# Attention over latent keys: who turns the exponentials, and a pool of large buffers cut in two

## The chip, the cores and the metric

The kernel runs on one core of a Trainium2 chip. The metric is the device time of one execution in microseconds (us); lower is better. All data are float32. For the large products an operand is split into two float32r parts, high and low (`hi = round(x)`, `lo = x - hi`), and a product is made of three matmuls: hi by hi, hi by lo, lo by hi.

The engines, by the names that the profile uses: PE (TensorE, matmuls; PEld is its loading of weights), DVE (VectorE), ACT (ScalarE), POOL (GpSimd), SP (SyncE, which issues most DMAs here). Each takes its own instructions strictly in the planned order. PSUM holds what TensorE writes; SBUF holds the tiles that the others work on; DRAM is reached by DMA only.

## What is computed

One layer of a diffusion backbone over 1024 latent tokens and 256 context tokens of width 1024: a SwiGLU FFN, then a short convolution beside grouped-query attention, merged and projected, then a second FFN, each with a modulated RMS norm. The change lies in the attention of the latent tokens, cut here to what matters:

```python
N_Q_HEADS, N_KV_HEADS, HEAD_DIM, SEQ, CTX_LEN = 8, 2, 128, 1024, 256

def gqa_attend(q, k, v):
    s = jnp.einsum('btkgd,blkd->bkgtl', q, k, preferred_element_type=jnp.float32) * (HEAD_DIM ** -0.5)
    p = jax.nn.softmax(s, axis=-1).astype(v.dtype)
    return jnp.einsum('bkgtl,blkd->btkgd', p, v)

k_all = jnp.concatenate([k_c, k_l], axis=1)   # 256 context keys, then 1024 latent keys
v_all = jnp.concatenate([v_c, v_l], axis=1)
o_l = latent_attention(q_l, k_all, v_all)     # 128 queries at a time
```

Per head and query there are 1280 keys: ten blocks of 128, two of the context and eight latent ones.

## The kernel before, in words

**Stages.** The first FFN (in a Winograd-like form that makes seven products of eight), the mixed projections, heads (q, k, v with norm and rotary), the attention stage, the merge and output projection, the second FFN, the final norm. A planner orders each engine's instructions: it takes the program's order as priority, but when an instruction isn't ready by its estimate of the times, a later one that is ready goes first. Waits are put in afterwards.

**Units.** Attention works in 16 units, one for each of 8 heads and 2 halves of the queries (512 each, four tiles `qt` of 128). `Unit.scores(qt)` makes the scores of one query tile: queries on the partitions, keys along the row, 256 of the context into half a bank and two banks of 512 for the latent keys. VectorE takes the row maxima (`m`, `nm`), ScalarE writes the exponentials, for the context into `pc` and for the latent keys into a tile `pl` of [128, 1024] for each query tile, and their sums into `rs`, which VectorE adds up into `rsum`.

**The second product.** It contracts over the keys, so the exponentials must have keys on the partitions. `Unit.turn(kt)` does that for one key block: four TensorE transposes, one for each query tile, into one PSUM bank `pt`; then `split` makes the two parts in a tile `pts` (ScalarE's cast for the high part, VectorE's subtraction for the low one). `Unit.values(kt, pts)` adds three matmuls of 512 columns to the bank `po`. `Unit.inverse` (at the fifth value step) takes the reciprocals of the sums and brings them, by two DMAs of POOL's queue through DRAM (`rinvd`, `rrow`), into a row that stands on all partitions. `Unit.output` copies `po` and lets POOL multiply it by that row.

**The order.** `seconds()` is a generator over all units and key blocks: each step turns one block, and once more than AHEAD (3) turned blocks wait, it multiplies the oldest. The loop over `units[1:]` issues a unit's `scores` and between them ten steps of the previous unit (`run(rest, 1)`), and steps of `fillers()`: the convolution branch's output projection (`conv_out`, with weights `wc` loaded and split by `conv_weights`, the subtraction on POOL), which is used up after about eleven units. In the last three units `split_output` puts casts and subtractions (`oh`, `ol`) of finished heads on POOL. After the loop the remaining steps run beside the first `merge` steps.

**Buffers.** Large tiles (4 KB on each partition) come from one pool of A_BUFS = 38 slots (`atile`): the residual stream, kept operands, k, v, q, the exponentials `pc` and `pl`, and so on. Split weights and `pts` take turns in four slots of the tag `wh`; small [128, 512] tiles come from `ttile` (11 slots).

A helper class records all engine calls, so that nearly all rows of the profile have the line L90; the names of the tiles tell them apart.

Of the kernel before, what the change touches and what calls it, by code (L numbers as in the profile page):

```python
# [37 lines left out]
A_BUFS = 38  # L38
W_BUFS = 4
AHEAD = 3  # L40
# [11 lines left out]
def tile_dit_layer(  # L52
# [52 lines left out]
    dram = ctx.enter_context(tc.tile_pool(name="dram", bufs=1, space=DRAM))  # L105

# [6 lines left out]
    def atile(name, shape=(P, SLOT), dt=F32):  # L113
        return apool.tile(list(shape), dt, tag="A", name=uniq(name))

# [291 lines left out]
    class Latents:  # L407


        def __init__(self, name):  # L410
            self.name, self.t = name, {}

        def pair(self, k, i):
            if (k, i) not in self.t:
                self.t[k, i] = atile(self.name, (P, 2, 512))
            return self.t[k, i]
# [6 lines left out]
    class Context:  # L423
        def __init__(self, name, dt=F32):
            self.t = [atile(name, (P, 4, CT), dt) for _ in range(2)]
# [66 lines left out]
    class Winograd:  # L492
# [6 lines left out]
        def __init__(self, xs, gain, mod, m, pairs, plain=False, ahead=3, side_from=None):  # L499
# [12 lines left out]
            self.source, self.ready = self.lefts(pairs, side_from), []  # L512

        def keep(self, i, k, src, lo_eng=None):

            t = atile(f"r{i}", (P, 2, 512), F32R)
            split(src, t[:, 0], t[:, 1], lo_eng)
            self.r[i][k] = t
# [38 lines left out]
        def norm1(self, turned=None):  # L557
# [8 lines left out]
            def scaled(k):  # L566
                t22[k] = ttile("h22")
                if self.plain:
                    self.r[0][k] = atile("h12", (P, 2, 512))
                    t12[k] = self.r[0][k][:, 0]  # L570
# [26 lines left out]
        def part_second(self, k):  # L597

            t = self.r[0][k]
            h = atile("r0", (P, 2, 512), F32R)  # L600
            split(t[:, 0], h[:, 0], h[:, 1])
# [133 lines left out]
        def start_by_half(self):  # L735

            uc = [atile("uc", (P, 2, 512)) for _ in range(2)]
# [96 lines left out]
    def row_products(w, rows, add, after=lambda i, k: None, halves=False):  # L834
# [12 lines left out]
        s1, s2, w11 = {}, {}, {}  # L847
# [13 lines left out]
        def parts(src, where):  # L861
# [3 lines left out]
            else:  # L865
                if where == "kept":
                    t = atile("kept", (P, 2, 512), F32R)
# [19 lines left out]
        def second_sum(k, m):  # L887
            s2[k] = atile("ws", (P, 2, 512))[:, :m]
# [3 lines left out]
        def sums(i, g):  # L892
# [11 lines left out]
            if i == 1 and g >= 3 or i == 4 and g < n - 3:  # L904
                k, m = groups[g - 3 if i == 1 else n - 3 + g]
                s1[k] = atile("ws", (P, 2, 512))[:, :m]
# [94 lines left out]
    xs, xc = Latents("x"), Context("xc")  # L1001

    def fetch_tokens(ch):
# [3 lines left out]
        for j in range(n // P):  # L1007
            t = atile("xtok")
# [166 lines left out]
    def side(j, bank=ps_o):  # L1175
        pc = bank()

        def do(i, w):
# [9 lines left out]
            if i == 4:  # L1188
                if j % 2 == 0:
                    hid_c[j // 2] = atile("hidc", (P, 4, CT), F32R)  # L1190
# [45 lines left out]
    for j in range(NH):  # L1236
# [6 lines left out]
        if j == SIDE_FROM - 1:  # L1243
# [10 lines left out]
            for token in range(2):  # L1254
                c_acc.append(atile("cacc"))
# [31 lines left out]
    xs = Latents("x1")  # L1287
# [116 lines left out]
    rope_t = [atile("rope", (P, KD, HD)) for _ in range(2)]  # L1404
    for i in range(2):
        sp.dma_start(out=rope_t[i][:], in_=rope[i])
    hg = atile("hg", (P, 2, HD))
# [171 lines left out]
    class Unit:  # L1579
# [3 lines left out]
        def begin(self):  # L1583
# [3 lines left out]
            self.pl = []  # L1587
            self.rsum = small("rsum", 4)

        def scores(self, qt):  # L1590
# [7 lines left out]
            m3, nm, rs = small("m3", 3), small("nm", 1), small("rs", 3)  # L1598
            dve.reduce_max(out=m3[:, 0:1], in_=sx, axis=AX.X)
            if self.hd == 0 and self.ch[1] == 0 and qt < 2:  # L1600
                pl = wpool.tile([P, SLOT], F32, tag="raw", name=uniq("pl"), bufs=3)
            else:
                pl = atile("pl")
            self.pl.append(pl)
            for j in range(2):
# [4 lines left out]
                parts.append((pl[:, j * 512 : (j + 1) * 512], ps))  # L1610
            dve.tensor_reduce(out=nm[:], in_=m3[:], axis=AX.X, op=ALU.max, negate=True)
            for j, (dst, ps) in enumerate(parts):
                act.activation(out=dst, in_=ps, func=AF.Exp, bias=nm[:], accum_out=rs[:, j : j + 1])
            dve.reduce_sum(out=self.rsum[:, qt : qt + 1], in_=rs[:], axis=AX.X)

        def turn(self, kt):

            pt = ps_t()
            for qt in range(4):
                src = self.pc[:, qt, kt * P : (kt + 1) * P] if kt < 2 else self.pl[qt][:, (kt - 2) * P : (kt - 1) * P]  # L1620
                transpose(pt[:, qt * P : (qt + 1) * P], src)
            pts = wpool.tile([P, 2, 512], F32R, tag="wh", name=uniq("pts"), bufs=W_BUFS)
            split(pt, pts[:, 0], pts[:, 1])
# [11 lines left out]
        def inverse(self):  # L1635
            rinv = small("rinv", 4)
# [6 lines left out]
        def output(self):  # L1643
            of = q_of(self.hd, self.ch)
            act.copy(out=of, in_=self.po)
            pool.tensor_mul(out=of, in0=of, in1=self.rows)

    def seconds():

        turned = []  # L1650
# [9 lines left out]
        for u in units:  # L1660
            for kt in range(10):
                turned.append((u, kt, u.turn(kt)))
# [3 lines left out]
        while turned:  # L1666
# [6 lines left out]
    def merge(j, ch):  # L1673

        if j not in m_hi:
            m_hi[j], m_lo[j] = atile("mh", dt=F32R), atile("ml", dt=F32R)
# [18 lines left out]

# [216 lines left out]
```

## Time and profile before

Three runs: 2631.09, 2631.25 and 2631.54 us, median 2631.25 us. The profiled execution:

| | |
|---|---|
| span | 2631.1 us |
| PE busy | 99% |
| DVE / ACT / POOL busy | 76% / 45% / 21% |
| granted TensorE clock | 0.998 |
| first and last transpose of `pl` start | 1462.6 us, 1808.7 us |
| number of `pl` transposes | 512 |
| number of splits into `pts` | 160 |
| DMA, mean over the span | 146 GB/s |

A row of instructions reads: line, engine, operation, output <- inputs by the program's names, shape, count | busy us, mean ns of one | idle time of the engine just before them, and what ended it. A row of the timeline reads: start (us), duration (us), engine, line, operation, output <- inputs, count, and in brackets the idle time before. PE durations run from issue to a modelled end and overlap; the distance from start to start is the slot that an instruction takes.

### The profile page before, as it was taken

The page shows a single profiled execution, that of the slowest core. Times are in us where ns is not written, and L with a number is a line of the kernel's source. Part 1 is how long each engine was busy: PE and PEld are TensorE (multiplying, and loading weights), DVE is VectorE, ACT ScalarE, POOL GpSimd, SP SyncE. Part 2 cuts the span into 40 slices and gives each one's busy share as a digit, 9 for nine tenths or more (in the row PEclk, how much of TensorE's full clock was granted, in tenths as well). Part 3 has the DMA queues.
Part 4 walks back from the last instruction along what each step waited for, and adds up shares of the span by engine and source line. Part 5 has one row for each costly group of instructions (what it writes and reads, how often), then busy time and mean ns, then how long its engine had stood idle before and what let it go on. Part 6 is the DMA issues. An engine that isn't in the chain of part 4 may idle for free.

```text
span 2631.1 us, 35379 instructions
## 1 busy us (share of the span) xinstructions
PE 2609.9 (99%) x12665; PEld 2176.1 (83%) x12665; DVE 1997.4 (76%) x3360; ACT 1183.5 (45%) x2343; POOL 545.8 (21%) x425
## 2 busy tenths in 40 slices
PE   8999999999999999999999999999999999999998
PEld 5888899888888888888888888888888888888888
DVE  5888976877897879977788576676457886667996
ACT  6533454333454642333355566574237333334553
POOL 0133201221010034333022112132000442321100
PEclk9999999999999999999999999999999999999999
DMA  8665465345973365542522322113425653227831
GB/s 324 205 210 182 149 215 173 106 131 185 327 184 117 124 205 160 163 134 89 200 77 85 86 87 65 33 37 118 158 85 176 201 167 96 90 80 286 191 84 65
DMA packets 372905, 384.69 MB, mean 146 GB/s; under 512 B 19686, under 2 KB 256376, under 8 KB 372728
## 3 DMA queue, kind: packets, MB, share of 16 engines
q1 hardware_dynamic: 363288, 363.52, 42.1%
q0 software_dynamic: 9440, 18.91, 4.3%
q8 instruction: 99, 1.62, 0.2%
q14 instruction: 78, 0.64, 0.1%
HBM read 310.45 MB, written 71.86 MB: 145 GB/s over the span
## 4 chain that ended last, share of the span: by engine, by line
PE 94%; DVE 3%; DMA 1%; ACT 1%; issue 1%; SPq 0%; DVEq 0%; ACTq 0%
PE ps L90 81%; PE pt L90 8%; PE po L90 6%; DMA rawm<-in_w_mod_dram 1%; DVE xb L90 0%; DVE wl L90 0%; DVE macc L90 0%; DVE m L90 0%; DVE y L90 0%; DVE pts L90 0%; DMA xtok<-in_x_dram 0%; DVE x L90 0%; DVE r L90 0%; SPq L90 0%; DVE rs_t L90 0%
## 5 line engine op out<-in xcount | busy, mean ns | idle before, releaser
L90 PE MATMUL ps<-r,wl 128*128 128x512 f32 x5196 | 1198.3, 390 | 3.6 <-ACT r L90 1.3
L90 PEld LDWEIGHTS ps<-r,wl 128*128 128x128 f32 x5196 | 972.4, 188 | 207.7 <-ACT r L90 1.6
L90 ACT CAST wl<-sum 128x512 fp32r<-128x512 f32 x218 | 134.1, 622 | 294.4 <-PE ps L90 227.1
L90 ACT CAST wl<-raw 128x512 fp32r<-128x512 f32 x287 | 178.2, 622 | 193.1 <-PE ps L90 147.9
L90 DVE TENSOR_TENSOR wl<-raw,wl 128x512 fp32r<-128x512 f32 x287 | 210.2, 736 | 61.0 <-ACT wl L90 59.3
L90 DVE TENSOR_TENSOR wl<-sum,wl 128x512 fp32r<-128x512 f32 x218 | 196.9, 904 | 33.5 <-ACT wl L90 32.3
L90 POOL TENSOR_TENSOR sum<-raw 128x512 f32<-128x512 f32 x55 | 76.4, 1389 | 680.6 <-DMA raw<-in_ffn_w_in_dram 345.3
L90 DVE SCALAR_TENSOR_TENSOR macc<-rawm,silu_c,macc 128x512 f32<-128x512 f32 x178 | 145.4, 835 | 17.1 <-DMA rawm<-in_w_mod_dram 16.6
L90 DVE TENSOR_TENSOR u<-u,ps 128x512 f32<-128x512 f32 x186 | 126.5, 680 | 32.2 <-PE ps L90 32.1
L90 ACT CAST rh<-hid 128x512 fp32r<-128x512 f32 x132 | 82.2, 623 | 139.4 <-PE ps L90 112.3
L90 POOL TENSOR_TENSOR sum<-raw,sum 128x512 f32<-128x512 f32 x55 | 76.7, 1395 | 287.0 <-DVE wl L90 284.0
L90 DVE TENSOR_TENSOR pts<-pt,pts 128x512 fp32r<-128x512 f32 x160 | 107.3, 686 | 36.2 <-ACT pts L90 34.6
L90 DVE TENSOR_REDUCE m<-ps 128x1 f32<-128x256 f32 (+1 forms) x192 | 111.0, 597 | 29.4 <-PE ps L90 28.5
L90 ACT CAST pts<-pt 128x512 fp32r<-128x512 f32 x160 | 92.2, 597 | 85.5 <-PE pt L90 84.4
L90 PE MATMUL ps<-rh,wl 128*128 128x512 f32 x360 | 122.8, 390 | 0.0
L90 PE MATMUL ps<-wh,r 128*128 128x512 f32 x384 | 120.7, 392 | 0.0
L90 DVE TENSOR_TENSOR rl<-hid,rh 128x512 fp32r<-128x512 f32 x132 | 91.0, 693 | 29.9 <-ACT rh L90 19.4
L90 ACT CAST wh<-raw 128x512 fp32r<-128x512 f32 (+1 forms) x85 | 68.2, 803 | 95.5 <-PE ps L90 74.9
L90 PE MATMUL ps<-kl,qs 128*128 128x512 f32 x384 | 104.0, 394 | 0.1
L90 PE MATMUL ps<-rh,wh 128*128 128x512 f32 x300 | 102.8, 389 | 0.0
L90 PE MATMUL ps<-y,wc 128*128 128x512 f32 x384 | 95.3, 391 | 0.2 <-DVE g L90 0.2
L90 POOL TENSOR_TENSOR sum<-sum,raw 128x512 f32<-128x512 f32 x55 | 87.8, 1597 | 5.7 <-PE ps L90 3.9
(325 smaller groups left out, 5102.3 us busy)
## 6 DMA issues: line engine op xcount, KB each, us to landing
raw<-in_ffn_w_in_dram SPq DMA_DIRECT2D x131, 512.0 KB
raw<-in_ffn_w_out_dram SPq DMA_DIRECT2D x72, 512.0 KB
raw<-in_w_in_dram SPq DMA_DIRECT2D x64, 512.0 KB
rawm<-in_w_mod_dram SPq DMA_DIRECT2D x104, 256.0 KB
hid<-hd SPq DMA_DIRECT2D x40, 512.0 KB
ucd<-uc SPq DMA_DIRECT2D x33, 512.0 KB
rawm<-in_w_mod_dram SPq DMA_DIRECT2D x32, 512.0 KB
ws<-in_ffn_w_out_dram POOLq DMA_DIRECT2D x26, 512.0 KB, 6.4
```

Of the source, the lines that this page charges most:

```text
L90: inst = getattr(self.engine, name)(*args, **kw)
```

## The change

The exponentials of the latent keys are no longer turned by TensorE.

- `Unit.begin` takes two tiles `pl` of [128, 2048], one for each half of the latent keys. The exponentials are written so that in each tile 32 keys of query tile 0 are followed by the same 32 keys of query tiles 1, 2 and 3, then the next 32 keys.
- `Unit.bring(kt)`: for the two context blocks the four TensorE transposes as before. For every second latent block one VectorE transpose in place over [128, 1024], which turns each 32x32 block by itself; four SP DMAs (one for each 32 partitions) write the result to a DRAM tile in pieces of 128 floats; and for each block one SP DMA reads 256 KB back into a `ttile`, now with keys on the partitions.
- `Unit.turn(kt, pt)` makes the split. For the context blocks the casts and subtractions reorder the columns as well; for the latent blocks they read SBUF, and the subtractions of blocks 3, 5, 6, 7 and 9 are on POOL.
- `seconds()` has one more queue: more than BROUGHT (3) blocks are brought before the oldest is split, and AHEAD is 2.
- The four sums `rsum` are made by one VectorE instruction in `inverse`; `output` copies with reordered columns.
- The pool of 38 slots becomes one of 30 and a second of 8, in the memory of which four slots of 8 KB (for `pl`) lie during attention (`share`). Outside attention a number of tiles take their slots from the second pool by name (`btile` in place of `atile`); in the mixed stage two `h12` share one tile.

```diff
-A_BUFS = 38
+A_BUFS, B_BUFS, Q_BUFS = 30, 8, 4
 W_BUFS = 4
-AHEAD = 3
+AHEAD = 2
+BROUGHT = 3
...
+    def share(tag, bufs):
+
+        if shared:
+            shared.pop("guard").__exit__(None, None, None)
+        guard = tc.tile_pool(name=uniq("share"), bufs=bufs, reuse_waits="tile")
+        shared.update(guard=guard, pool=guard.__enter__(), tag=tag)
...
+    def btile(name, shape=(P, SLOT), dt=F32):
+        return shared["pool"].tile(list(shape), dt, tag=shared["tag"], name=uniq(name))
...
             self.pc = atile("pc", (P, 4, CT))
-            self.pl = []
-            self.rsum = small("rsum", 4)
+            self.pl = [btile("pl", (P, 2048)) for _ in range(2)]
+            self.done = 0
+            self.rs, self.rsum = small("rs", 12), small("rsum", 4)
...
-                parts.append((pl[:, j * 512 : (j + 1) * 512], ps))
+                pl = self.pl[j][:].rearrange("p (b q c) -> p b q c", q=4, c=32)
+                parts.append((pl[:, :, qt], ps.rearrange("p (b c) -> p b c", c=32)))
...
-                act.activation(out=dst, in_=ps, func=AF.Exp, bias=nm[:], accum_out=rs[:, j : j + 1])
-            dve.reduce_sum(out=self.rsum[:, qt : qt + 1], in_=rs[:], axis=AX.X)
-
-        def turn(self, kt):
-
-            pt = ps_t()
-            for qt in range(4):
-                src = self.pc[:, qt, kt * P : (kt + 1) * P] if kt < 2 else self.pl[qt][:, (kt - 2) * P : (kt - 1) * P]
-                transpose(pt[:, qt * P : (qt + 1) * P], src)
+                at = 3 * qt + j
+                act.activation(out=dst, in_=ps, func=AF.Exp, bias=nm[:], accum_out=self.rs[:, at : at + 1])
+            self.done += 1
+
+        def bring(self, kt):
+
+            if kt < 2:
+                pt = ps_t()
+                for qt in range(4):
+                    transpose(pt[:, qt * P : (qt + 1) * P], self.pc[:, qt, kt * P : (kt + 1) * P])
+                return pt
+            pl, k = self.pl[(kt - 2) // 4], (kt - 2) % 4
+            if k % 2 == 0:
+                part = pl[:, k * 512 : (k + 2) * 512]
+                dve.transpose(out=part, in_=part)
+                self.turned = dram.tile([8, 32, 4, P], F32, name=uniq("ptd"))
+                for i in range(4):
+                    sp.dma_start(
+                        out=self.turned[:, :, i].rearrange("j r f -> r j f"),
+                        in_=part[i * 32 : (i + 1) * 32].rearrange("r (j f) -> r j f", j=8),
+                    )
+            raw, at = ttile("pt"), k % 2 * 4
+            sp.dma_start(out=raw, in_=self.turned[at : at + 4].rearrange("j r i f -> (j r) (i f)"))
+            return raw
+
+        def turn(self, kt, pt):
+
             pts = wpool.tile([P, 2, 512], F32R, tag="wh", name=uniq("pts"), bufs=W_BUFS)
-            split(pt, pts[:, 0], pts[:, 1])
+            if kt < 2:
+                v = lambda t: t.rearrange("p (i q c) -> p q i c", i=4, q=4)
+                u = pt.rearrange("p (q i c) -> p q i c", i=4, q=4)
+                act.copy(out=v(pts[:, 0]), in_=u)
+                dve.tensor_sub(out=v(pts[:, 1]), in0=u, in1=v(pts[:, 0]).bitcast(F32))
+            else:
+                split(pt, pts[:, 0], pts[:, 1], pool if kt % 2 or kt == 6 else dve)
             return pts
...
         def inverse(self):
+            dve.reduce_sum(out=self.rsum[:], in_=self.rs[:].rearrange("p (q j) -> p q j", j=3), axis=AX.X)
...
-            act.copy(out=of, in_=self.po)
+            v = lambda t, by: t.rearrange(by, i=4, q=4)
+            act.copy(out=v(of, "p (q i c) -> p q i c"), in_=v(self.po, "p (i q c) -> p q i c"))
...
             for kt in range(10):
-                turned.append((u, kt, u.turn(kt)))
+                brought.append((u, kt, u.bring(kt)))
+                if len(brought) > BROUGHT:
+                    parts()
                 if len(turned) > AHEAD:
                     value()
...
+    share("Q", Q_BUFS)
     units = [Unit(hd, ch) for hd in range(NQ) for ch in (C0, C1)]
...
-    run(rest, 4)
+    run(rest, BROUGHT + AHEAD + 1)
...
     split_output(NQ - 1, C1, late=True)
+    share("B", B_BUFS)
...
-    xs = Latents("x1")
+    xs = Latents("x1", 3)
```

72 lines of the change are left out of this document (40 added, 32 removed).

## The prediction

> **What bounds the kernel now.** I read the page first (parts 1 and 4), then the stretch of the span in which the change works, by the windows view.
>
> ```profile
> span 2631.1 us, 35379 instructions
> PE 2609.9 (99%) x12665; PEld 2176.1 (83%) x12665; DVE 1997.4 (76%) x3360; ACT 1183.5 (45%) x2343; POOL 545.8 (21%) x425
> PE ps L90 81%; PE pt L90 8%; PE po L90 6%; DMA rawm<-in_w_mod_dram 1%; DVE xb L90 0%; DVE wl L90 0%; DVE macc L90 0%; DVE m L90 0%; DVE y L90 0%; DVE pts L90 0%; DMA xtok<-in_x_dram 0%; DVE x L90 0%; DVE r L90 0%; SPq L90 0%; DVE rs_t L90 0%
> 1440.00:1822.00 382.00, 378.65 (x2057) 316.02 (x2056) 250.92 (x536) 237.10 (x593) 88.63 (x85) 1.00 0.24 65
> 1440.00:1711.00 271.00, 268.76 (x1448) 224.37 (x1447) 175.61 (x380) 165.87 (x418) 49.50 (x41) 1.00 0.25 69
> 1711.00:1822.00 111.00, 109.89 (x612) 91.65 (x611) 75.30 (x158) 71.24 (x177) 39.13 (x44) 1.00 0.21 56
> ```
>
> The last three lines give the attention stage, then its two parts (eleven units with other matmuls between them, and five without): length, then busy time of PE, PEld, DVE, ACT, POOL, the granted clock, the DMA share and GB/s. TensorE is idle for 382 - 378.65 = 3.4 us of the stage, and for 21.2 us of the span; its clock is full. DVE is at 66%, ACT at 62%, POOL at 23%, the DMA engines at 24%. So TensorE's instruction stream is the bound, and an instruction taken from it shortens the kernel by its whole slot until one of the others takes over. The span is 0.2 us under the median of the runs (2631.25), so I reckon from the span. About 0.2% (5 us) is what a measurement of this kernel can tell from no change.
>
> **What leaves TensorE.** Eight of the ten key blocks of each of 16 units stop being turned by it.
>
> ```profile
> L90 PE MATMUL pt<-ident,pl 128*128 128x128 f32 x512 | 76.6, 273 | 1.5 <-DVE pts L90 1.4
> ...
> 1614.91 0.39 PE L90 MATMUL po<-pts,vl 128*128 128x512 f32 x1
> 1615.14 0.39 PE L90 MATMUL po<-pts,vh 128*128 128x512 f32 x1
> 1615.37 0.60 PE L90 MATMUL pt<-ident,pl 128*128 128x128 f32 x4
> 1615.72 0.49 PE L90 MATMUL po<-pts,vh 128*128 128x512 f32 x1
> 1616.05 0.39 PE L90 MATMUL po<-pts,vl 128*128 128x512 f32 x1
> 1616.28 0.40 PE L90 MATMUL po<-pts,vh 128*128 128x512 f32 x1
> ```
>
> The 273 ns of one transpose is a pipelined time, not its slot; slots are read from start to start. From 1615.14 to 1616.28 lie three 512-column matmuls and four transposes: 1.14 us. A matmul alone takes 1615.14 - 1614.91 = 0.23 us, so four transposes cost 1.14 - 0.69 = 0.45 us. 512/4 x 0.45 = 57.6 us, or 3.6 us a unit. That is the gain if nothing else ends late: 325 us for the stage, and 2573.5 us.
>
> **What VectorE gets.** It loses the low parts of five blocks a unit (80, to POOL) and 48 of its 64 small sums, and gains four 128x1024 transposes a unit (64).
>
> ```profile
> L90 DVE TENSOR_TENSOR pts<-pt,pts 128x512 fp32r<-128x512 f32 x160 | 107.3, 686 | 36.2 <-ACT pts L90 34.6
> L90 DVE TENSOR_REDUCE rsum<-rs 128x1 f32<-128x3 f32 x64 | 9.8, 153 | 45.5 <-ACT pl L90 44.9 <-issue 0.5
> L90 DVE TENSOR_TENSOR hid<-hid,hid 128x1024 f32<-128x1024 f32 x60 | 73.3, 1226 | 0.0
> L90 DVE TENSOR_SCALAR xtok<-xtok,rs_y 128x1024 f32<-128x1024 f32 x6 | 4.2, 750 | 0.8 <-PE po L90 0.7
> ```
>
> No transpose by VectorE is in the trace. The nearest rows of its size are 0.75 us (one input) and 1.23 us (two); I take 1.23, since a block transpose has to fill before it drains, and twice that, 2.45, as the upper end. Removed: 80 x 0.686 + 48 x 0.153 = 62.2 us. Added: 64 x 1.23 = 78.7 us. VectorE then has 250.9 - 62.2 + 78.7 = 267 us of 325, 82%: not the bound. At 2.45 us it would have 346 us and bind by 21 us; the switch is at 2.13 us. [...]
>
> **What ScalarE gets.** The same number of casts; those of the latent blocks read SBUF and not PSUM.
>
> ```profile
> L90 ACT CAST pts<-pt 128x512 fp32r<-128x512 f32 x160 | 92.2, 597 | 85.5 <-PE pt L90 84.4
> L90 ACT CAST qs<-q 128x512 fp32r<-128x512 f32 x15 | 9.4, 629 | 6.4 <-DVE xb L90 6.4
> ```
>
> 128 x (629 - 597) = 4 us more, 241 of 325 us. The exponentials now land in runs of 32 values, and 32 casts read in four dimensions; I price both at nothing. If strides cost a fifth of 160 x 0.6, 19 us, ACT stays at 80%: its slack covers it.
>
> **What POOL gets, and the wait in its queue.** 80 subtractions come to an engine that stands in order behind a DMA each unit.
>
> ```profile
> L90 POOL TENSOR_TENSOR ol<-q,oh 128x512 fp32r<-128x512 f32 x14 | 17.9, 1286 | 0.0
> L90 POOL DMA_DIRECT2D rrow<-rinvd x16 | 9.1, 571 | 123.3 <-DMA rinvd<-rinv 96.2 <-PE pt L90 18.6 <-issue 8.5
> ...
> 1754.54 0.79 POOL L90 DMA_DIRECT2D rinvd<-rinv  x1
> 1755.34 1.31 POOL L90 TENSOR_TENSOR ol<-q,oh 128x512 fp32r<-128x512 f32 x1
> 1763.32 0.58 POOL L90 DMA_DIRECT2D rrow<-rinvd  x1 [6.67 <-DMA rinvd<-rinv]
> 1763.89 1.18 POOL L90 CAST oh<-q 128x512 fp32r<-128x512 f32 x2
> ```
>
> The subtractions are 80 x 1.29 = 103 us. The second row says more: before each of 16 broadcasts (`rrow`) POOL stands idle, 123.3/16 = 7.7 us, until the reciprocals (`rinvd`) have landed. The timeline shows that the planned order puts one instruction under that cover and leaves others (`oh`) behind it, although they need nothing of it: the plan thinks the landing earlier than it is. Until now that idle time cost nothing. Now the low parts `pts`, which TensorE's value matmuls read, queue behind it. In the late part POOL would have 39.1 + 5 x 7.7 + 25 x 1.29 = 110 us of work and waits in place of 111 - 5 x 3.6 = 93 us: 17 us short, or 4 us if two subtractions a unit (13 us) fall under the waits. I take 10 us lost there. In the early part it has 49.5 + 11 x 7.7 + 55 x 1.29 = 205 us in 271 - 11 x 3.6 = 231, so only the order hurts: a subtraction behind `rrow` comes up to 8.8 - 1.3 = 7.5 us late (1754.54 to 1763.32, less one sheltered), against AHEAD and the four `pts` buffers, two to three steps of (378.65 - 57.6)/160 = 2.0 us. Ends are 0 and 3.5 us a unit; I take 1 us, 11 us in all.
>
> **What the DMA engines get.** Per unit 2.1 MB goes out in pieces of 512 B and comes back in rows of 2 KB: 33.5 MB each way.
>
> ```profile
> 1519.50:1522.50 3.00, 3.00 (x22) 2.68 (x21) 2.29 (x7) 3.00 (x8) 0.00 (x0) 1.00 1.00 367
> DMA packets 583, 1.10 MB, mean 367 GB/s; under 512 B 75, under 2 KB 75, under 8 KB 583
> 1447.90:1448.70 0.80, 0.80 (x5) 0.64 (x5) 0.00 (x0) 0.80 (x3) 0.00 (x0) 1.00 1.12 329
> DMA packets 516, 0.26 MB, mean 329 GB/s; under 512 B 2, under 2 KB 516, under 8 KB 516
> ```
>
> Each pair is one stretch in which the engines are full, the first with 2 KB packets and the second with 512 B ones (loads): 367 and 329 GB/s (294 if the share of 1.12 is taken out). So 33.5/367 + 33.5/294 = 91 + 114 = 205 us, beside 0.24 x 382 = 92 us of now: 297 of 325 us, 91%. Not the bound, but transfers will queue, the fillers' weights among them; I take 5 us for that (0 to 31, the upper end being the half-rate rival's below).
>
> **The way round, and SP.** From transpose to matmul a block now passes VectorE, a write, a read and a split.
>
> ```profile
> DMA to landing us min/median/max: 3.5/4.0/7.1
> 1620.97 0.26 ACT L90 ACTIVATION_READ_ACCUMULATOR pl<-ps,nm 128x1 f32 x1
> 1621.45 0.18 DVE L90 RECIPROCAL rinv<-rsum 128x4 f32<-128x4 f32 x1
> 1439.76 0.38 SPq L90 DMA_DIRECT2D raw<-in_w_branch_conv_dram  x1
> ```
>
> The first line is that of `rrow`, a 256 KB transfer. 1.23 + 4.0 + 4.0 + 0.63 + 1.29 = 11.2 us, against BROUGHT + AHEAD = 5 steps of 2.0 us. But the planner doesn't wait for a step's place in the text: the reciprocals, written at the fifth value step, run 0.2 us after the unit's last exponential, so I expect the transposes as early, and no loss in the middle. SP issues 24 more DMAs a unit, 24 x 0.38 = 9 us of 20, in order: reads that wait for writes stand before the loads `raw<-in_w_branch_conv` and `g<-gcd`, which conv_out's matmuls need. That is covered while those are planned a unit ahead; if not, it shows as PE waiting for `wc`. At the end of the stage no later unit covers the last one's 11.2 us, only the merges; I take 3 us (0 to 11).
>
> **Other stages.** 30 + 8 slots are the same bytes as 38, but a tile can now only take a slot of its own pool. TensorE's 21.2 - 3.4 = 17.8 us of idle time outside the stage is what can shrink or grow; I take 0, with -3 and +6 as ends.
>
> **Sum.** 2631.1 - 57.6 + 10 + 11 + 5 + 3 = 2602.5, say 2602 us. With every loss at its lower end (4 late, none else) it is 2577.5; with half more loss than I take it is 2617.
>
> **Rivals.**
> *Everything is covered (0.18).* TensorE keeps its 99%, the subtractions fall under the waits. For it: all four other resources sum to under 92% of 325 us. Against it: POOL's 7.7 us per unit. 2570 to 2580 us, at best the 57.6 us and the 3.4 us of idle time: 2570.
>
> *The writes run at half rate (0.14).* Each write leaves from 32 partitions only, where every transfer of the rows above has 128. If those reach half the paths, 33.5/184 = 182 us in place of 114, and the engines have 182 + 91 + 92 = 365 us, the bound of the stage: 2631 - 382 + 365 = 2614 us; beside reads on the other half it may be nearer the forecast. The traces bear out neither. [...]
>
> *POOL's queue holds TensorE (0.20, slower).* The place is a low part `pts` behind `rrow`, each unit. `rinvd` is small packets; beside engines 91% full its landing grows (by `rinvd`'s and `rrow`'s rows it now takes 8 to 12 us).
>
> ```profile
> DMA to landing us min/median/max: 3.5/7.5/12.1
> ```
>
> (That is the row of the tile `rinvd`, both DMAs together.) With 12 us and slack of 4 to 6, TensorE loses 4 to 7 us of its 3.6 us gain in each unit. It decides from 3.6 us a unit on: at 5 us, 16 x 5 - 57.6 = +22 us, 2653 us; at 4 us, 2637.
>
> *It cancels (0.08).* Losses of 3.3 to 3.9 us a unit: 2626 to 2636 us.
>
> **How the numbers follow.** Forecast 0.40 (own range 2583 to 2620), covered 0.18, half rate 0.14: faster by over 0.2% 0.72; within 0.2% 0.08; slower 0.20. The range runs from 2572, just above full cover, to 2642, and leaves out the far end of the slower case and the last microseconds of full cover, together under 0.2.
>
> **What would show it.** Right: no `pt<-ident,pl` rows, 64 VectorE transposes near 1.2 us, a DMA share near 0.9 between 1440 and the stage's end, `rrow` still preceded by idle POOL, and TensorE's new idle time (20 to 35 us) put down to POOL `pts`, most of it late. Wrong: TensorE idle under 8 us (covered); its waits ending on `pt` loads, or writes under 200 GB/s (half rate); a POOL `pts` wait of over 3.6 us a unit; VectorE above 95% in the stage (transposes over 2.1 us); or a difference outside the stage of more than 6 us.

## The result and the profile after

The kernel with the change takes 2783.77 us (median of 4 runs, 2779.83 to 2789.4), the kernel before beside it on the same chip 2631.39 us (4 runs, 2631.09 to 2633.26). The ratio is 1.0578, 95% interval 1.0563 to 1.0593: 152 us slower, where 2602 us and a gain were forecast. It lies outside the range of 2572 to 2642 us as well.

The page of the kernel after: its first line, the busy times, the clock in 40 slices, and the start of the shares of its chain by line.

```profile
span 2780.5 us, 35121 instructions
...
PE 2626.3 (94%) x12153; PEld 2159.7 (78%) x12153; DVE 2029.9 (73%) x3296; ACT 1189.2 (43%) x2343; POOL 651.8 (23%) x505
...
PEclk9999999999999999999998888888999999999999
...
PE ps L91 43%; DMA ptd<-pl 5%; DMA pt<-ptd 5%; PE pt L91 2%; SPq L91 1%; PE po L91 1%; DVE pl L91 1%; DVE m L91 0%; ACT pts L91 0%; DVE xb L91 0%; DVE pts L91 0%; POOL pts L91 0%; DVE y L91 0%; ACT pc L91 0%; ACT pl L91 0%
```

TensorE executes 512 instructions fewer and yet is busy 16 us longer. Its clock dips where the attention stage lies, and the two DMAs of the new way, which the kernel before did not have, hold 5% of the chain each. The windows view parts the span into what is before, in and behind the stage (length; then busy PE, PEld, DVE, ACT, POOL; clock; DMA share; GB/s). First the kernel before, ahead of its stage and behind it, then the kernel after:

```profile
0.00:1430.00 1430.00, 1420.18 (x6852) 1182.37 (x6852) 1163.78 (x1949) 625.98 (x1216) 311.69 (x237) 1.00 0.53 171
1822.00:2631.00 809.00, 801.07 (x3711) 669.32 (x3709) 575.33 (x864) 314.68 (x524) 145.50 (x104) 1.00 0.46 141
```
```profile
0.00:1430.00 1430.00, 1420.23 (x6837) 1182.66 (x6838) 1160.19 (x1945) 624.60 (x1216) 310.42 (x236) 1.00 0.53 171
1440.00:1970.00 530.00, 393.56 (x1553) 298.07 (x1553) 286.38 (x475) 245.69 (x596) 194.12 (x164) 0.86 0.71 171
1970.00:2780.00 810.00, 802.70 (x3719) 670.99 (x3717) 575.36 (x866) 315.18 (x525) 145.85 (x104) 1.00 0.46 142
```

Outside the stage nothing moved by more than 2 us. The stage alone went from 382 to 530 us, 148 of the 149 us between the spans. In it no engine is full: TensorE is idle for 136 us and has a granted clock of 0.86, VectorE is at 54%, the DMA engines at 71%. So what grew is mostly waiting. The groups of the stage, and then the waits of ScalarE, TensorE and POOL (us in total, times, longest), say who waits for whom:

```profile
L91 DVE STREAM_TRANSPOSE pl<-pl 128x1024 f32<-128x1024 f32 x64 | 74.6, 1215 | 17.3 <-ACT pl L91 11.9 <-DMA pt<-ptd 5.4
...
L91 POOL TENSOR_TENSOR pts<-pt,pts 128x512 fp32r<-128x512 f32 x80 | 105.3, 1323 | 173.9 <-ACT pts L91 157.5
...
L91 ACT CAST pts<-pt 128x512 fp32r<-128x512 f32 x160 | 95.9, 615 | 226.7 <-DMA pt<-ptd 187.7
...
L91 PE MATMUL ps<-kl,qs 128*128 128x512 f32 x384 | 128.7, 460 | 21.8 <-DVE g L91 10.4
```
```profile
ACT pts L91 <- DMA pt<-ptd: 187.7, 56, 7.7
...
PE ps L91 <- ACT pc L91: 51.1, 19, 7.3
PE po L91 <- ACT pts L91: 31.0, 13, 5.8
...
PE ps L91 <- POOL pts L91: 4.7, 4, 3.1
PE po L91 <- POOL pts L91: 3.6, 7, 0.8
...
POOL rrow L91 <- DMA rinvd<-rinv: 29.3, 3, 11.6
```

ScalarE stands for 187.7 us at casts of blocks that have not come back from DRAM. Behind such a cast in its queue stand the exponentials; they hold the PSUM banks that the next scores need, and TensorE's longest wait is for those (`ps` for ACT `pc`, 51.1 us). The wait that the prediction feared most, TensorE for POOL's low parts, is 8.3 us in all (the value steps of some units write to a bank named `ps`, those of the others to `po`).

**Why the blocks come late.** Three windows of one unit in the columns of above, and the three rows of the timeline that matter to them; the reciprocals' store is issued at 1628.47:

```profile
1622.00:1632.00 10.00, 6.35 (x29) 4.94 (x27) 7.02 (x12) 3.51 (x7) 4.42 (x3) 0.92 0.81 235
1632.00:1639.00 7.00, 4.63 (x14) 3.53 (x14) 3.22 (x7) 1.21 (x5) 0.00 (x0) 0.63 0.95 67
1645.00:1652.00 7.00, 5.97 (x30) 4.43 (x28) 3.40 (x5) 3.34 (x8) 3.82 (x3) 1.00 0.99 328
```
```profile
1621.48 4.61 DVE L91 STREAM_TRANSPOSE pl<-pl 128x1024 f32<-128x1024 f32 x4
...
1622.74 4.33 SPq L91 DMA_DIRECT2D ptd<-pl  x7
...
1628.47 0.78 POOL L91 DMA_DIRECT2D rinvd<-rinv  x1 [5.18 <-PE ps L91]
```

`rinvd` writes 512 reciprocals (2 KB) to DRAM, by the program as 512 pieces of 4 bytes; the profile has the store as 32 packets of queue q0. For seven microseconds, from 3.5 us after its issue on, the DMA engines are 95% busy and move 67 GB/s, all of it packets of the other queue (q1: 981 packets, 0.47 MB); a little later, at 99%, they move 328 GB/s. The unit's four VectorE transposes run in one burst right before, so the store falls among the writes and reads that the unit needs. The store is issued once in each of 16 units, and this unit is not alone. Cut into windows of 2 us, the stage of the change has 19 in which the engines are at least 80% busy and yet move under 130 GB/s; the stage of the kernel before has none. Over the whole stage the change moves 171 GB/s with the engines 71% busy, and the first run below, which leaves the store out, 197 GB/s with the engines 66% busy. The store stands in the kernel before as well, but there TensorE is idle for only 3.4 us of the stage.

### The profile page after: what moved, and what is told of

Same layout as the page of the kernel before. It is cut to its first block, busy times and chain, and to the rows that moved or that the text cites. A ratio compares the mean times of both kernels' runs of the same rounds, so it can differ in the third digit from the quotient of the medians.

```text
span 2780.5 us, 35121 instructions
## 1 busy us (share of the span) xinstructions
PE 2626.3 (94%) x12153; PEld 2159.7 (78%) x12153; DVE 2029.9 (73%) x3296; ACT 1189.2 (43%) x2343; POOL 651.8 (23%) x505
## 4 chain that ended last, share of the span: by engine, by line
PE 47%; DMA 10%; DVE 3%; issue 1%; SPq 1%; ACT 1%; POOL 1%; DVEq 0%; ACTq 0%; POOLq 0%
PE ps L91 43%; DMA ptd<-pl 5%; DMA pt<-ptd 5%; PE pt L91 2%; SPq L91 1%; PE po L91 1%; DVE pl L91 1%; DVE m L91 0%; ACT pts L91 0%; DVE xb L91 0%; DVE pts L91 0%; POOL pts L91 0%; DVE y L91 0%; ACT pc L91 0%; ACT pl L91 0%
## 5 line engine op out<-in xcount | busy, mean ns | idle before, releaser
L91 DVE TENSOR_TENSOR wl<-raw,wl 128x512 fp32r<-128x512 f32 x287 | 206.1, 721 | 57.6 <-ACT wl L91 56.1
L91 ACT CAST pts<-pt 128x512 fp32r<-128x512 f32 x160 | 95.9, 615 | 226.7 <-DMA pt<-ptd 187.7
L91 DVE TENSOR_REDUCE m<-ps 128x1 f32<-128x512 f32 (+1 forms) x192 | 110.9, 593 | 77.0 <-PE ps L91 76.9
L91 PE MATMUL ps<-kl,qs 128*128 128x512 f32 x384 | 128.7, 460 | 21.8 <-DVE g L91 10.4
L91 POOL TENSOR_TENSOR pts<-pt,pts 128x512 fp32r<-128x512 f32 x80 | 105.3, 1323 | 173.9 <-ACT pts L91 157.5
L91 DVE TENSOR_TENSOR pts<-pt,pts 128x512 fp32r<-128x512 f32 x80 | 61.5, 775 | 90.3 <-ACT pts L91 90.0
L91 PEld LDWEIGHTS ps<-kl,qs 128*128 128x128 f32 x384 | 80.7, 225 | 44.7 <-DVE g L91 13.0
```

Of the source, the lines that this page charges most:

```text
L91: inst = getattr(self.engine, name)(*args, **kw)
```

## The experiments

All times are medians, beside 2631 to 2633 us of the kernel before. The expectations name theories by letters. In short: **S**, the store of the reciprocals slows all transfers, and the new way depends on them (**S2**: store and way together are all of the loss); **L**, the way through DRAM is long whatever the store does, and ScalarE stands at its blocks; **P**, POOL's subtractions behind its waits; **B**, at first, the reshaped buffers and strided writes themselves (further below the letter stands for something else); **R**, the rate of the transfers; **C**, something that computes, not a transfer, and there **V**, VectorE's transposes, against **O**, the order of the other steps.

**Without the store (S).** The reciprocals are turned by TensorE in place of the two DMAs; all else stays.

```diff
-            row = dram.tile([512], F32, name=uniq("rinvd"))
-            pool.dma_start(out=row.rearrange("(j p) -> p j", p=P), in_=rinv[:])
+            pr = ps_t()
+            for j in range(4):
+                transpose(pr[:, j * P : (j + 1) * P], rinv[:, j : j + 1].to_broadcast([P, P]))
...
-            pool.dma_start(out=self.rows, in_=row.partition_broadcast(P))
+            act.copy(out=self.rows, in_=pr)
```

> The change as it is, but the reciprocals reach all partitions by four TensorE transposes of a broadcast column and one ScalarE copy; the two POOL DMAs (rinvd, rrow) are gone. Theory S (the small store): rinvd, a store in pieces of 4 bytes, slows all transfers for 7 to 8 us in each of 16 units, and the new way through DRAM now waits for them; without it 2784 - 16 x 7.5 = 2664 us, 2640 to 2690. Theory L (the way round is too long): bursts of 2 MB out and back and a plan that thinks them shorter hold ScalarE's casts whatever rinvd does; 2760 to 2795 us. Theory P (the prediction's rival, POOL's queue): the wait of rrow goes, but TensorE waits for POOL's pts for only 8 us in the trace; 2770 to 2780 us.

2688.48 us (2686.76 to 2693.2), ratio 1.0213 [1.0196, 1.023]: in S's range. The store, together with the 256 KB that `rrow` reads back, cost 95 us, after what the transposes in its place take. ScalarE's wait falls from 187.7 to 77.9 us, and the stage to some 440 us:

```profile
ACT pts L91 <- DMA pt<-ptd: 77.9, 35, 6.4
```
```profile
1440.00:1880.00 440.00, 370.24 (x1624) 287.86 (x1623) 285.69 (x475) 252.70 (x611) 176.07 (x133) 0.92 0.66 197
```

**The store twice (S).**

```diff
+            for _ in range(2):
+                row = dram.tile([512], F32, name=uniq("rinvd"))
+                pool.dma_start(out=row.rearrange("(j p) -> p j", p=P), in_=rinv[:])
```

> The change as it is, with the store rinvd issued twice in each unit into two DRAM rows, of which the second is read. S: another 6 to 8 us a unit, 2784 + 16 x 7 = 2896 us, 2860 to 2920. L: 16 x 0.8 us of POOL at most, 2784 to 2800 us. P: rrow waits some 3 us longer in each unit, 2790 to 2830 us.

2885.35 us (two runs), ratio 1.0958 [1.0936, 1.098]: another 102 us, in S's range. The number fits S, but the trace shows a second road. POOL stands idle before the second store, which sets the low parts behind it in its queue back, and TensorE's wait for POOL's low parts rises from 8.3 to 94.4 us:

```profile
PE po L91 <- POOL pts L91: 48.5, 13, 9.0
PE ps L91 <- POOL pts L91: 45.9, 9, 13.1
...
POOL rinvd L91 <- issue: 118.7, 12, 11.1
```

ScalarE's wait for blocks rises too, from 187.7 to 237.4 us. So this run shows that a store is dear here, not that all of its price is slower transfers.

**Without the way through DRAM, with the store.** The turned block is split where it stands.

```diff
                 dve.transpose(out=part, in_=part)
-                self.turned = dram.tile([8, 32, 4, P], F32, name=uniq("ptd"))
...
-            raw, at = ttile("pt"), k % 2 * 4
-            sp.dma_start(out=raw, in_=self.turned[at : at + 4].rearrange("j r i f -> (j r) (i f)"))
-            return raw
+            return pl[:, k * 512 : (k + 1) * 512]
```

> The write to DRAM and the read back are left out: the splits read the block transposed by VectorE straight from SBUF, so the keys of the latent blocks are not in their places; everything else of the change stays, rinvd and rrow too. S and L: nothing on TensorE's path passes the DMA engines, so the stage falls to TensorE's work: 2575 to 2600 us. P: the subtractions on POOL still stand behind rrow: 2600 to 2650 us. Theory B (the reshaped buffers or the strided writes cost the time): over 2700 us.

2707.58 us, ratio 1.0283 [1.0265, 1.03]: over 100 us beyond what S and L expected and 58 beyond P, in the range of B, the reshaped buffers, which a run of their own below speaks against. So the way through DRAM is not the whole. Two rows of the waits:

```profile
POOL rrow L91 <- DMA rinvd<-rinv: 100.8, 15, 10.1
...
PE po L91 <- POOL pts L91: 25.6, 9, 8.4
```

Here, without the traffic, the POOL rival of the prediction does appear: POOL waits for the reciprocals in 15 units, and TensorE nine times for a low part of POOL.

**Without both.**

> Both left out: the way through DRAM (keys of the latent blocks not in their places) and the two POOL DMAs of the reciprocals (four TensorE transposes and a ScalarE copy instead). Theory S2: the 76 us that stayed when only the way through DRAM was gone are POOL's low parts behind the wait of rrow, so they go: 2575 to 2600 us. Theory C: the chain of split and value matmuls with POOL in it, or the planned order, is slow by itself: 2660 us or more.

2658.02 us, ratio 1.0094 [1.0079, 1.0109]. Way and store together are 126 of the 152 us; 2658 is still 26 us over the kernel before, with no transfer left that the change brought. That is 2 us under C's range and far from S2's. The waits now end on VectorE and on exponentials that wait for row maxima (`nm`):

```profile
PE pt L91 <- DVE rinv L91: 23.1, 5, 6.7
PE ps L91 <- ACT pc L91: 10.1, 13, 1.7
...
ACT pc L91 <- DVE nm L91: 70.8, 31, 5.7
```

**The buffers alone.** Reshaped buffers and one sum for four tiles as in the change, but TensorE turns everything, with AHEAD 3 and nothing brought ahead.

> TensorE turns all ten blocks again, VectorE makes all low parts, no way through DRAM, AHEAD 3 and no BROUGHT; the reshaped buffers, the double tiles of the exponentials and the one sum stay. S, L and P: 2625 to 2640 us, as before the change. B: over 2650 us.

2642.66 us, ratio 1.0035 [1.0022, 1.0048]: 3 us above the range of S, L and P, and under B's. The part that was priced at nothing costs some 10 us; the windows put it in the stage, but which of its edits it is wasn't taken apart.

**More lookahead.** The kernel without the store, with BROUGHT 6 in place of 3.

> The reciprocals by TensorE, the way through DRAM kept, and BROUGHT 6 in place of 3. Theory L: the 56 us that stay over the time before are the latency of the way round against a reach of five steps; three steps more cover it: 2600 to 2650 us. Theory R (rate: the DMA engines, or SP's issues, can't carry 4.2 MB a unit faster): 2675 to 2700 us.

2683.89 us, ratio 1.0198 [1.0182, 1.0215]: 5 us less than with 3, and the two intervals overlap. It is R's range, and L's is missed by 34 us. The transposes follow the unit's exponentials in either case, in fours or in pairs. ScalarE's wait for blocks does fall, from 77.9 to 48.8 us, but TensorE's wait for banks that exponentials hold (`ps` for ACT `pc`) rises from 21.4 to 35.3 us: that wait alone is not what the way costs.

**Larger pieces.** The kernel without the store, each half megabyte written by one DMA in rows of 4 KB from all 128 partitions; the data stand in other places.

```diff
-                for i in range(4):
-                    sp.dma_start(
...
+                sp.dma_start(out=self.turned.rearrange("j r i f -> (j r i f)").rearrange("(p n) -> p n", p=P), in_=part)
```

> The reciprocals by TensorE, and each 512 KB written by one DMA in rows of 4 KB from 128 partitions instead of four DMAs in pieces of 512 B from 32 partitions each; the same bytes go out and come back, but not to their places, so the output is not the reference's. R (small pieces, 32 partitions, 192 more issues on SP): 2630 to 2660 us. L: one landing instead of four saves a little, 2670 to 2690 us.

2669.26 us, ratio 1.0137 [1.0122, 1.0152]. Small pieces, 32 partitions and three more issues for each half megabyte together cost 19 us. R's range was missed by 9 us, L's by 1 on its lower side: the form of the writes is a part of the way's price.

**Low parts back on VectorE (P).** The change with the store, no subtraction on POOL.

```diff
-                split(pt, pts[:, 0], pts[:, 1], pool if kt % 2 or kt == 6 else dve)
+                split(pt, pts[:, 0], pts[:, 1])
```

> The change as it is, with all low parts on VectorE and none on POOL; rinvd and rrow stay. Theory S: the small store still slows the transfers, 2765 to 2800 us. Theory P (low parts behind rrow hold TensorE in the change itself): 2700 to 2750 us.

2815.51 us, ratio 1.0693 [1.0671, 1.0714], 32 us slower than the change and 15 us above S's range. P is refuted for the change itself: with no low part on POOL the loss does not shrink, and ScalarE's wait for the same blocks is longer (221.1 us). That VectorE's added work does the harm is likely, not shown.

**Transposes spread out (V against O).** Each VectorE transpose is kept in the program's order, two steps apart, first without transfers and store, then with the transfers (and BROUGHT 5).

```diff
-                dve.transpose(out=part, in_=part)
+                tc.keep_in_program_order(dve.transpose(out=part, in_=part))
```

> As the run with neither the way through DRAM nor POOL's two DMAs, but each transpose is kept behind all VectorE instructions that stand before it in the program, so that the four of a unit are two steps apart. V: the burst was the harm, 2590 to 2635 us. O: 2650 to 2670 us.

> The whole change with the reciprocals by TensorE, the transposes kept in the program's order, and BROUGHT 5 so that the way round, which now begins later, has seven steps. V: 20 to 50 us under the 2688 us of the floating transposes, 2640 to 2668 us. L: the way round begins later and holds ScalarE's casts more, 2690 to 2740 us.

2657.59 us, ratio 1.0096 [1.0079, 1.0113]: the same as with the burst, as O has it. And 2752.97 us, ratio 1.0457 [1.0441, 1.0472]: 64 us worse than with the burst, L's direction and 13 us beyond L's range. ScalarE waits 98.1 us for blocks there (77.9 with the burst). So the burst isn't the harm; with the transfers, beginning late is.

**Half of it.** Without the store, only the latent blocks 6 to 9 go the new way; TensorE turns 2 to 5.

> The reciprocals by TensorE, and only the latent blocks 6 to 9 go the new way; blocks 2 to 5 are turned by TensorE. If costs and gains are shares of the blocks, the middle between the run with all eight (2688 us) and all by TensorE with 7 us for the reciprocals (2650 us): 2660 to 2675 us. V and L: a burst of two transposes and half the traffic fit into the slack, and the gain of 29 us on TensorE shows: 2610 to 2640 us.

2642.47 us, ratio 1.0038 [1.0023, 1.0053], between the two ranges: the time of the buffers alone (2642.66). It takes 256 transposes, some 29 us, from TensorE and gives it some 7 us of turning reciprocals, so that 22 us of gain should show beside the buffers alone, and none does.

**Without the transposes (V).** As without both, and the latent exponentials are neither turned nor placed.

> As the run with neither the way through DRAM nor POOL's two DMAs, and VectorE's transposes left out too: the latent exponentials are split as they lie, neither turned nor placed. Theory V: what is left of the loss is VectorE, where the plan runs a unit's four transposes in one burst of 4.6 us ahead of maxima and low parts that TensorE's next work waits for; without them 2575 to 2610 us. Theory O: it is the order of the splits, with POOL in the chain; 2640 us or more.

2625.03 us (2623.96 to 2626.59), ratio 0.9971 [0.9959, 0.9983]. The transposes cost 33 us, but the 57.6 us that TensorE was spared still do not come out: it lies between V's range and O's. The stage, then a wait of TensorE and one of VectorE:

```profile
1440.00:1815.00 375.00, 346.89 (x1606) 276.88 (x1605) 220.16 (x409) 247.46 (x608) 180.11 (x132) 0.97 0.15 50
```
```profile
PE ps L91 <- ACT pc L91: 17.4, 14, 2.5
...
DVE m L91 <- PE ps L91: 84.1, 74, 4.5
```

TensorE is idle for 28 us at a clock of 0.97. VectorE has less to do than before the change (220 us of 375, then 251 of 382), so its load as a whole is not it. TensorE waits for a bank of scores whose exponentials are not made, while VectorE waits for scores. That is a chain that goes in a circle: scores, row maxima, exponentials, bank free, next scores. Two theories were left. **M**: that chain is what is late next. **B**: the low parts on POOL and the order of the value steps are.

> The same kernel (2625 us) with the maxima, but all low parts on VectorE, none on GpSimd; latent exponentials still neither turned nor placed. Theory B: without GpSimd's 1.3 us per subtraction the steps run on time, 2590 to 2610 us. Theory M: VectorE has more to do ahead of the maxima, 2630 to 2660 us.

All low parts on VectorE: 2615.67 us, ratio 0.9937 [0.992, 0.9953]. Only 9 us better, between the two ranges: POOL's slower subtractions are a small part.

The maxima are then left out of four kernels; the edit is the same in each:

```diff
-            dve.reduce_max(out=m3[:, 0:1], in_=sx, axis=AX.X)
...
-                dve.reduce_max(out=m3[:, j + 1 : j + 2], in_=ps, axis=AX.X)
...
-            dve.tensor_reduce(out=nm[:], in_=m3[:], axis=AX.X, op=ALU.max, negate=True)
+            dve.memset(nm[:], -1.0)
...
-                act.activation(out=dst, in_=ps, func=AF.Exp, bias=nm[:], accum_out=self.rs[:, at : at + 1])
+                act.activation(out=dst, in_=ps, func=AF.Exp, bias=nm[:], scale=0.01, accum_out=self.rs[:, at : at + 1])
```

> The kernel without VectorE's transposes, the way through DRAM and the reciprocals' row (2625 us), and now also without the row maxima: the exponentials take a constant bias and a scale of 0.01, so the softmax is another one; their number and size stay. Theory M: TensorE's remaining idle time (28 us in the stage, 17.4 us of it waiting for a score bank that an exponential holds, while ScalarE waits 46 us for the maxima) comes from the chain scores, maxima, exponentials, on which the VectorE work for the low parts lies too. Then 2580 to 2600 us. Theory B: the low parts on GpSimd and the order of the steps hold it; then 2615 to 2630 us.

> Control: the kernel before without the row maxima (constant bias, scale 0.01, another softmax). Both theories: TensorE's instructions bind there and its idle time in the stage is 3.4 us, so 2625 to 2633 us. If it is faster by more than 6 us, the chain of the maxima cost the kernel before as well, and M's gain in the other run has to be reduced by as much.

> The kernel with VectorE's transposes, but without the way through DRAM and with the reciprocals turned by TensorE (2658 us), now without the row maxima (constant bias, scale 0.01, another softmax; the keys are not in place either). Theory M: the transposes cost time because the maxima stand behind them in VectorE's queue; without maxima 2585 to 2610 us. Theory B: the transposes lie on the way of the value steps themselves; 2635 to 2660 us.

Without VectorE's transposes 2588.02 us, ratio 0.9834 [0.982, 0.9849]; with them 2587.70 us, ratio 0.9836 [0.9821, 0.9851]; the kernel before 2633.97 us, ratio 1.0004 [0.9995, 1.0014]. The first two lie in M's ranges, the control 1 us above its own: the maxima cost the kernel before nothing, and in the other two they hide the gain. Without them the 64 transposes are free. The stage with the transposes, and then the stage of the change with and without the store in the two runs that follow:

```profile
1440.00:1778.00 338.00, 332.49 (x1625) 274.05 (x1624) 190.87 (x283) 250.90 (x608) 179.35 (x133) 0.99 0.18 57
```
```profile
1440.00:1905.00 465.00, 371.10 (x1542) 289.13 (x1541) 194.59 (x279) 238.54 (x587) 193.29 (x164) 0.88 0.84 194
```
```profile
1440.00:1810.00 370.00, 343.49 (x1622) 274.81 (x1621) 188.61 (x283) 247.48 (x605) 177.95 (x133) 0.99 0.79 233
```

> The kernel after, all of it (2784 us), without the row maxima (constant bias, scale 0.01, another softmax). Theory M has explained the last two losses: without maxima neither VectorE's transposes nor the rest cost anything over the TensorE floor. If the wait of ScalarE for the blocks that come back from DRAM costs time only by that chain as well, 2600 to 2660 us. Theory L: ScalarE stands in order at the casts of blocks that have not landed, and with it the exponentials, whatever the maxima do, and the slow transfers after each store of the reciprocals remain: 2700 to 2760 us.

> The kernel after with the reciprocals turned by TensorE, so without the store (2688 us), also without the row maxima (constant bias, scale 0.01, another softmax). M alone: 2588 to 2600 us, like the kernel without the way through DRAM. L: the 30 us that the way through DRAM cost remain, 2610 to 2640 us.

2719.53 us, ratio 1.0341 [1.0322, 1.0361], and 2621.38 us, ratio 0.9959 [0.9944, 0.9973]: L's ranges. Leaving out the maxima doesn't remove the loss by late transfers. In the change without maxima ScalarE still stands at its blocks for 133 us:

```profile
ACT pts L91 <- DMA pt<-ptd: 133.2, 46, 9.3
```

Medians in us, put together:

| | with maxima | without | difference |
|---|---|---|---|
| kernel before | 2632 | 2634 | none |
| without transposes, DRAM way and store | 2625 | 2588 | 37 |
| without DRAM way and store | 2658 | 2588 | 70 |
| without store | 2688 | 2621 | 67 |
| the change | 2784 | 2720 | 64 |

Down either column, in this order, the way through DRAM costs 30 or 34 us and then the store 95 or 98; across, the chain of the maxima costs 64 to 70 us once the transposes are in. So the maxima's loss and the transfers' loss add. Store and way don't add: each makes the other dearer. By the run with the store and without the way (2708 us), the store costs 50 us where there is no way, and the way costs 76 us where the store is in. The DMA engines show it as well. Without the way, with and without the store:

```profile
1440.00:1900.00 460.00, 369.07 (x1541) 288.20 (x1540) 296.05 (x474) 241.62 (x593) 192.66 (x165) 0.88 0.21 50
```
```profile
1440.00:1850.00 410.00, 355.98 (x1631) 282.31 (x1631) 285.14 (x475) 250.60 (x611) 180.32 (x133) 0.95 0.15 49
```

There the store and its reading back keep the engines busy for 0.21 x 460 - 0.15 x 410 = 35 us; beside the way, for 0.71 x 530 - 0.66 x 440 = 86 us. No kernel of these runs that still computes the layer was faster than the kernel before; the nearest are the buffers alone and the half.

## Why the prediction was wrong

**The gain was about right.** 57.6 us of TensorE's slots were forecast. Without the maxima, the way through DRAM and the store the stage takes 338 us. The predicted floor was 325, to which that kernel adds 7 us for turning the reciprocals (16 x 0.45); 6 us remain, and the buffers may be in them.

**"I take 5 us for that (0 to 31)", the DMA engines' queueing, failed, and it is the largest miss.** 297 us of busy engines were forecast, and without the store and the maxima the window shows 0.79 x 370 = 292 us. That is closer than the sum deserves, since the 297 us have the store and its reading back in them. With the store it is 0.71 x 530 = 376 us, 84 us or 5 us a unit more. A stretch such as the one shown is of that size: 7 us at 67 GB/s are 0.47 MB, for which 1.4 us at 328 GB/s would do, and the engines were busy for 6.7. The prediction also has 31 us, its upper end, as the half-rate rival's loss; by its own figures that would be 365 - 325 = 40. The prediction had `rinvd`'s row before it and asked only how late the store itself would land beside full engines; what it does to the transfers beside it wasn't asked. In place of 5 us it was 95.

**"No loss in the middle", the way round, failed.** 11.2 us against five steps of 2.0 us counted every step of the way at its undisturbed time. The planner did put the transposes right behind the exponentials, as expected. Even without the store ScalarE waits 77.9 us for blocks, and this way costs 30 to 34 us in place of none. Of it some 19 us go with the writes' form. SP's order, which the prediction took as covered, shows a little: TensorE waits 10.6 us for the fillers' `g` in the change, though only 3.0 us of VectorE's wait there end on the load `g<-gcd`. The half-rate rival wanted 365 us of busy DMA engines; the 292 us without the store and the maxima leave no room for it. That writes from 32 partitions reach half the paths was the author's supposition, and no run timed such a write by itself: four of them, each from other 32 partitions, went out beside one another.

**"Not the bound", VectorE at 82%, failed as a reason.** The transposes' price was right (1.23 us taken, 1.215 measured), in part by luck, since it came from another operation; that a block has to fill before it drains, the reason given for it, no run shows. VectorE's total was 20 us too low (267 us forecast, 286 measured): the low parts left to it took 775 ns in place of 686, the group `qs<-q,qs` 1172 in place of 686. Still it is not full in the stage (54%). Yet VectorE's maxima stand in a circle with PSUM's banks, and a delay of them, or less work beside them, shows in the time. The waits of ScalarE in the stage of the kernel before had a row of it:

```profile
ACT pc L90 <- DVE nm L90: 39.6, 28, 3.1
```

ScalarE waited 39.6 us for `nm`, and TensorE had other work in each unit for that time. When the transposes left TensorE, that cover went: the maxima then cost 37 us without a single VectorE transpose and 70 us with them, against none in the kernel before. That is a rival that the prediction didn't have. The runs without maxima take away both the wait and VectorE's time for them, 121 us in the groups of the kernel without transposes:

```profile
L91 DVE TENSOR_REDUCE m<-ps 128x1 f32<-128x512 f32 x125 | 85.6, 687 | 55.9 <-PE ps L91 55.2
...
L91 DVE TENSOR_REDUCE m<-ps 128x1 f32<-128x256 f32 x63 | 26.1, 419 | 29.6 <-PE ps L91 28.9 <-ACT pts L91 0.4 <-ACT wc L91 0.2
...
L91 DVE TENSOR_REDUCE nm<-m 128x1 f32<-128x3 f32 x63 | 9.4, 150 | 1.0
```

So how much is the circle itself and how much VectorE's time in it stays open. For the circle speaks that VectorE was less loaded than before where 37 us were lost, and that more low parts on it did no harm there (2616 us). No run left the maxima out beside the buffers and the shorter AHEAD alone, so part of the 37 us may be theirs.

**POOL.** 1.29 us a subtraction was right (1.32), and so was POOL's total (88.6 + 103 = 192 us; 194.1 measured). The 21 us of loss by its queue are not there in the change: POOL's wait for `rinvd` is 29.3 us in three units, its wait for ScalarE's casts 157.5 us, and TensorE's wait for POOL 8.3 us. The mechanism is real in two other runs: without the way through DRAM (25.6 us of TensorE's idle time on `po`) and with the store doubled (94.4 us). The rival's forecast of "slower" has the sign, at a seventh of the size or less, and by another road from the same store.

**Small terms.** ScalarE 241 us forecast, 245.7 measured. Other stages 0 within -3 and +6: the windows outside agree within 2 us, but the buffers cost some 10 us in a run of their own, inside the stage, where the sum had no term for them. The 3 us for the end of the stage were not measured by themselves.

**What remains open.** Whether the store's harm lies in the number of its pieces, in their 4 bytes or in writing to DRAM: no run varied these. The store was not left out without `rrow`, its reading back, either. Nor was it tried to place the store before the unit's transfers.

## What to carry to other kernels

When the bounding engine loses instructions, a circle of dependencies that they covered can become the next bound, and busy shares don't show it: look in the trace of before for waits between the other engines (here ScalarE for the maxima, 39.6 us) and ask what fills the bounding engine meanwhile; test it by a run that leaves the dependency out. Before a chain is led through DRAM, list every small-piece DMA that is issued in the same stage, and count not only how late it lands but what it does to the transfers beside it (here 67 GB/s for 7 us behind a store of 2 KB).

## What the hardware showed

- In the change, behind a store of 512 values of 4 bytes and beside other transfers, the 16 DMA engines look 95% busy at 67 GB/s for 7 us (328 GB/s at 99% six microseconds later). A busy share is no rate.
- Over the attention stage of these runs the granted clock was the lower, the more of it TensorE was idle: 0.99 with 5.5 of 338 us idle, 0.97 with 28 of 375, 0.92 with 70 of 440, 0.86 with 136 of 530. In short windows it didn't go by the busy share alone: 0.92 where TensorE was busy for 6.35 of 10 us, 0.63 where it was busy for 4.63 of the next 7. In the stage of the change the group `ps<-kl,qs` shows 460 ns a matmul in place of 394, and TensorE is busy 16 us longer over the span with 512 instructions fewer: its stalls cost more than their own length (133 us more idle time in a stage that grew by 148 us).
- The VectorE transpose of 128x1024 float32 took 1215 ns in the change (1214 to 1223 in it and seven other runs), about as much as the two-input operation of that size that was taken for it (1226).
- Subtractions on VectorE that read SBUF had a longer tail than those that read PSUM: without transposes and transfers a mean of 957 ns (median 721, longest 1781) against 681 ns (longest 692), with part of such work on POOL. With none of it on POOL the mean of those that read SBUF was 789 ns (median 683, longest 2480).
